# A hybrid decoder layer: four edits of the mixers' order, and the second norm's transposes of token tiles 1 and 3 at other places

## The chip, the cores and the metric

The kernel runs on one core of a Trainium2 chip. The metric is the device time of one execution in microseconds (us). The kernel before took 745.96 us, the median of three runs (744.57 to 748.39). Five engines work side by side: PE multiplies matrices into PSUM banks, DVE, ACT and POOL do element-wise work, and SP issues the transfers (DMA).

## The reference

One layer of a decoder trunk for 512 tokens of 1024 features, in float32.

```
x1  = x  + gate1 * out_proj(concat(FoX, RWKV7, MoBA))    # of in_proj(adaLN(RMSNorm(x)))
x2  = x1 + gate2 * down(silu(conv3(up_g)) * conv3(up_v)) # of adaLN(RMSNorm(x1))
out = RMSNorm(x2)

FoX  : softmax(q k / 8 + F_t - F_s), causal, 4 heads of 64
RWKV7: S_t = S_(t-1) diag(w_t) - (S_(t-1) kk_t)(kk_t a_t)^T + v_t k_t^T,  y_t = S_t r_t, 8 heads of 64
MoBA : causal attention in the own block of 256 keys and in the best past blocks, 4 heads of 64
```

The adaLN shifts, scales and gates are products of a conditioning vector with weights of their own. The hidden width of the gated MLP is 2816.

## The kernel before

**Products.** A float32 product is made of three matmuls: weights and data are each split into a high and a low part, and high by high, low by high and high by low are summed in PSUM. The input projection is cut into *units* of one contraction step each (three matmuls, L459 to L461, 128x128 weights against 512 tokens), the output projection likewise (L957 to L959). The class `Feed` hands them out: `feed.run(n)` issues the next n units, `feed.until(name)` issues units until the chunk of that name is done. It runs ahead with the weights of the chunks that follow: a transfer to `w_st`, a cast on ACT (`w_hi`, L229) and a subtraction on POOL or DVE (`w_lo`, L231). With each unit it also takes one step off `feed.side`, the list of small jobs beside: `mod2_steps` (32 steps, each a transfer of `w_m` and a DVE multiply, L434), then for each half `gate_steps` (eight steps, DVE L412 and L414), `gate_parts` (L420, L421), three empty steps and `gate_end` (two matmuls, L425).

**RWKV preparation.** For four pairs of heads j, `norm_cols(j)` spreads the norms over the partitions (one matmul, L529) and `k_prep(j)` builds the operands on DVE, ACT and POOL: `kk` (L632), `kt` (POOL, L635), `av` (L636), the first half of `KR` (L637), the two halves of `BK` (L639, L642), `rk` (L641) and the second half of `KR` (L643). `k_cols(j, q)` scales `BK` on POOL (`BKs`, L653) and turns it on PE (L658). `grams(j, par)` multiplies `BK` by `KR` into two banks, `at` and `ch` (L672), and DVE masks each of them into `AG` (L674). In the loop over j stand, in this order, `r_prep` (L665), `k_cols(j, 0)`, `grams(j, 0)`, one unit, `k_cols(j, 1)`, `grams(j, 1)` and two units.

**Recurrence.** It goes over eight chunks `cc` of 64 tokens. In each, PE multiplies `AG` by the state `vs` (L1092), starts the outputs (L1098), solves (L1108; ACT and DVE L1110 copy the result), and makes the next state (L1118), which DVE adds per parity (L1121) before L1092 of the next chunk can start. Between these stand attention steps (scores L1001 to L1005 into `at` banks, softmax on DVE and ACT, turning on PE L1019 into `mm` banks, copied as `ptr` L1021) and units, by the list `PAT`: an attention step and a unit, the same again, one unit, nothing. The first unit of a tile takes a new `mm` bank, of which there are two, shared with L1019. After chunk 4 the MoBA heads begin, and their scores need all their queries and keys: `feed.until` then issues what is missing, and DVE forms the last piece (`mk`, L735).

**Second norm.** `tail` adds the last contraction steps of the output projection for one token tile (three matmuls a step). `norm2_sum` adds to the residual and scales the rows; `norm2_cols(i)` turns token tile i on PE (L1226, two `mm` banks), shifts and scales it on ACT (L1234) and DVE (L1231), casts the high part on ACT (L1238) and subtracts the low part on POOL (L1239). The first up products (`up`) take token tiles 0 and 1 for four row blocks into two `ch` and two `at` banks, then tiles 2 and 3: 16 matmuls with the high part of the data (L1430, L1431) and 8 with the low part (L1433), each of 256 columns.

**What sets the order.** In the mixers PE runs in the order in which the program is written; the order on the other engines is made by a scheduler from the data and from priorities. From the second norm's first step to the first up products all engines run in the written order.

Of the kernel before, what the change touches and what calls it, by code (L numbers as in the profile page):

```python
# [14 lines left out]
OP = mybir.AluOpType  # L15
# [53 lines left out]
MP = ['', '2', '2']  # L69
PT = 3  # L70
GE = 3

SEVEN = (7, 9, 11, 13, 15)
NA = 16
# [66 lines left out]
def hybrid_trunk(ctx, tc, x, vecs, convs, mod_cols, mod_gates, in_first, in_cols, in_fox, in_moba, fox_f_bias, lora,  # L141
# [350 lines left out]
    with mix:  # L492
# [38 lines left out]
        with tc.tile_pool(name="prep", bufs=1) as pp:  # L531
# [98 lines left out]
            def k_prep(j):  # L630
                kk[j] = pp.tile([P, T], F32, name="kk", bufs=1)
                V.scalar_tensor_tensor(kk[j], kt[j], col("k_k", j), pnr[j], op0=OP.mult, op1=OP.mult)  # L632
                t1 = pp.tile([P, T], F32, name="t1", tag="sq", bufs=SQ)
                S.activation(t1, av[j], AF.Identity, scale=col("k_a", j), bias=omka[:, j:j + 1])
                G.tensor_tensor(kt[j], kt[j], t1, op=OP.mult)  # L635
                V.tensor_tensor(av[j], av[j], kk[j], op=OP.mult)  # L636
                V.tensor_tensor(KR[:, j, :, 0, :], c3(kk[j]), Pv[j][:, :, 0:64], op=OP.mult)  # L637
                BK[j] = pp.tile([P, 8, 3, 64], F32, name=f"BK{j}")
                V.tensor_tensor(BK[j][:, :, 0, :], c3(av[j]), c3(sv[j]), op=OP.mult)  # L639
                rk[j] = pp.tile([P, T], F32, name="sq", bufs=SQ)  # L640
                V.scalar_tensor_tensor(c3(rk[j]), KR[:, j, :, 1, :], col("r_k", j), c3(kt[j]), op0=OP.mult, op1=OP.mult)  # L641
                V.tensor_tensor(BK[j][:, :, 1, :], c3(kt[j]), c3(sv[j]), op=OP.mult)  # L642
                V.tensor_tensor(KR[:, j, :, 1, :], KR[:, j, :, 1, :], Pv[j][:, :, 1:65], op=OP.mult)  # L643
                S.copy(BK[j][H[1], :, 2, :], BK[j][H[1], :, 0, :])
# [22 lines left out]
            def grams(j, par):  # L667
                r = slice(64 * par, 64 * par + 64)
                for q in range(2):
                    pg = bank("ch" if q else "at", [P, 4, 2, 64])  # L670
                    for z in range(4):
                        mm(pg[:, z, :, :], BK[j][r, 4 * q + z, par:par + 2, :], KR[r, j, 4 * q + z, :, :],  # L672
                           start=True, stop=True)
                    V.tensor_tensor(AG[:, par, j, 4 * q:4 * q + 4, :].rearrange("p c (a t) -> p c a t", a=2), pg,  # L674
                                    mask[:, None, :, :].to_broadcast([P, 4, 2, 64]), op=OP.mult)

                for blk in range(2):
                    b = block(par, blk)
                    S.copy(AA[b, j], AG[b, par, j, :, 32 * blk:32 * blk + 32])


            norm_cols(0)
            k_prep(0)
            feed.until("r3")
            feed.run(LEAD[0])
            norm_cols(1)
# [3 lines left out]
            for j in range(4):  # L690
# [3 lines left out]
                k_cols(j, 0)  # L694
                for n, step in enumerate((lambda: grams(j, 0), lambda: feed.run(F1), lambda: k_cols(j, 1),
                                          lambda: grams(j, 1), lambda: feed.run(F2[j]), lambda: None)):
                    if n == KO and j < 2:
                        norm_cols(j + 2)
                        k_prep(j + 2)
                    step()  # L700
# [376 lines left out]


        v_tiles(0)
        feed.side += mod2_steps(w_m) + [mod2_end]  # L1080
        for half in range(2):
            feed.side += gate_steps(0, half, macc2, w_m) + [lambda half=half: gate_parts(0, half, m_part)]
            feed.side += [lambda: None] * GE + [lambda half=half: gate_end(0, half, bank("at"), g1b)]
# [1 line left out]
        for cc in range(NC_):  # L1085
# [42 lines left out]
            if cc > 5:  # L1128
                bonus(2 * cc - 12)
                bonus(2 * cc - 11)  # L1130
            fill(PAT[3])
        turn_bank[0] = "ch"
        gn_var(0)
        feed.run(G1)
# [130 lines left out]
    norm2_sum(1)  # L1265
    tail(2, 4, 5, 6, 7)
    norm2_cols(0)
    tail(3, 4, 5, 6)
    norm2_cols(1)
    tail(3, 7)  # L1270
    norm2_sum(2)
    norm2_sum(3)
    feed.run(UP2)
# [177 lines left out]
    for h in range(2):  # L1451
        for n, pu in enumerate(pfirst):
            feed.run(max(0, 6 + 2 * n - len(kept)))
            up(pu, kept[4 + 2 * n:6 + 2 * n], slice(256 * h, 256 * h + 256))
            if h == 0 and n < 2:
                norm2_cols(2 + n)
    us[0] = [conv(pu, NF * n) for n, pu in enumerate(pfirst[:2])]
    LATE.close()
    mixers.close()
# [118 lines left out]
```

## Time and profile before

| | |
|---|---|
| median of three runs | 745.96 us |
| the profiled execution | 745.82 us |
| its span, first to last instruction | 744.0 us |
| busy time of PE, DVE, ACT, POOL | 716.1, 484.3, 365.0, 311.6 us |
| mean granted clock of PE | 0.978 of full speed |

All durations below come from the one profiled execution, whose span lies 1.8 us below its time. A timeline row tells the start, the length and the instruction, and in square brackets how long the engine had been idle and who ended that. PE's matmuls overlap, so the distance from one start to the next tells more than a row's length. [...]

### The profile page before, as it was taken

To read this page: it belongs to the slowest core of one execution; us is meant where nothing else is said; L and a number is where in the kernel's file an instruction comes from. 1 tells how busy PE (TensorE), PEld (TensorE's weight loads), DVE (VectorE), ACT (ScalarE), POOL (GpSimd) and SP (SyncE) were. 2 spreads that over 40 slices of the span, in tenths; PEclk is the share of its full clock that TensorE was granted. 3 is DMA by queue.
4 is the path that set the end of the run, shared out by engine and by line. 5 is a ranking of instruction groups with operands and counts; after the bars stand their busy time and mean duration, and the time that the engine had idled before them with its cause. 6 is when DMAs were issued, how large, how long until landed. Compare 5 with 4: busy or idle time off the path is not lost.

```text
span 744.0 us, 11850 instructions
## 1 busy us (share of the span) xinstructions
PE 716.1 (96%) x4404; PEld 570.2 (77%) x4404; DVE 484.3 (65%) x833; ACT 365.0 (49%) x714; POOL 311.6 (42%) x264
## 2 busy tenths in 40 slices
PE   7999999999997999999999999999999999999996
PEld 5874767897665766677788888888888888888884
DVE  7957996876987567742639796788757683114104
ACT  8748655454432553645566545565563353223204
POOL 0023854664442312636576745454475432225210
PEclk9999989999977999999999999999999999999998
DMA  8941201237754141115234314323156633322203
GB/s 329 399 156 42 69 19 30 86 100 231 239 170 143 35 152 44 57 52 172 74 102 126 114 28 111 104 93 92 43 141 199 215 100 109 99 87 97 102 1 113
DMA packets 43021, 86.93 MB, mean 117 GB/s; under 512 B 5002, under 2 KB 5204, under 8 KB 42964
## 3 DMA queue, kind: packets, MB, share of 16 engines
q1 hardware_dynamic: 42963, 86.18, 36.0%
q8 instruction: 34, 0.56, 0.3%
q14 instruction: 24, 0.19, 0.1%
HBM read 84.05 MB, written 2.10 MB: 116 GB/s over the span
## 4 chain that ended last, share of the span: by engine, by line
PE 69%; DVE 15%; ACT 6%; issue 4%; POOL 3%; DMA 2%; SPq 0%; ACTq 0%; POOLq 0%; DVEq 0%
PE mm L459 3%; PE mm L460 3%; PE mm L461 2%; PE ch L378 2%; POOL w_lo L231 2%; PE ch L1188 2%; PE ch L1189 2%; PE ch L1187 2%; PE at L1315 2%; PE ch L1315 2%; PE at L1318 2%; PE at L1316 2%; DMA w_st<-in_w_up_dram 2%; PE ch L1318 2%; PE ch L1316 2%
## 5 line engine op out<-in xcount | busy, mean ns | idle before, releaser
L231 POOL TENSOR_TENSOR w_lo<-w_st,w_hi 128x512 fp32r<-128x512 f32 (+1 forms) x162 | 225.4, 1400 | 322.7 <-ACT w_hi L229 299.6
L229 ACT CAST w_hi<-w_st 128x512 fp32r<-128x512 f32 (+1 forms) x199 | 121.6, 618 | 157.1 <-PE at L1189 46.1
L231 DVE TENSOR_TENSOR w_lo<-w_st,w_hi 128x512 fp32r<-128x512 f32 x39 | 32.4, 832 | 72.8 <-ACT w_hi L229 72.7
L459 PE MATMUL mm<-h_hi,w_hi 128*128 128x512 f32 x104 | 49.4, 475 | 1.4 <-ACT ptr L1021 1.4
L460 PE MATMUL mm<-h_lo,w_hi 128*128 128x512 f32 x104 | 42.6, 410 | 0.0
L461 PE MATMUL mm<-h_hi,w_lo 128*128 128x512 f32 x104 | 42.6, 410 | 0.0
L1315 PE MATMUL ch<-h_hi,w_hi 128*128 128x512 f32 (+1 forms) x100 | 35.4, 363 | 0.7 <-ACT tm L1378 0.7
L1316 PE MATMUL ch<-h_hi,w_lo 128*128 128x512 f32 (+1 forms) x100 | 35.2, 361 | 0.0
L434 DVE SCALAR_TENSOR_TENSOR w_m<-w_m,cB 128x512 f32<-128x512 f32 x32 | 27.6, 886 | 9.3 <-DMA w_m<-in_mod_cols_dram 9.2
L1315 PE MATMUL at<-h_hi,w_hi 128*128 128x512 f32 (+1 forms) x88 | 32.4, 375 | 0.2 <-ACT tm L1378 0.2
L1316 PE MATMUL at<-h_hi,w_lo 128*128 128x512 f32 (+1 forms) x88 | 32.2, 372 | 0.0
L1008 DVE TENSOR_REDUCE mx<-at 128x1 f32<-128x128 f32 (+3 forms) x32 | 15.6, 488 | 18.9 <-PE at L1005 18.7
L1010 ACT ACTIVATE pr<-at,mx 128x128 f32<-128x128 f32 (+3 forms) x32 | 16.9, 527 | 21.8 <-DVE mx L1008 21.3
L459 PEld LDWEIGHTS mm<-h_hi,w_hi 128*128 128x128 f32 x104 | 20.6, 198 | 8.9 <-issue 3.1
L1444 ACT ACTIVATE tm<-tm 128x512 f32<-128x512 f32 x22 | 13.9, 632 | 27.5 <-DVE tm L1439 27.5
L1315 PE MATMUL mm<-h_hi,w_hi 128*128 128x512 f32 (+1 forms) x72 | 27.2, 382 | 0.0
L1316 PE MATMUL mm<-h_hi,w_lo 128*128 128x512 f32 (+1 forms) x72 | 27.1, 380 | 0.0
L461 PEld LDWEIGHTS mm<-h_hi,w_lo 128*128 128x128 f32 x104 | 20.6, 198 | 5.0
L1318 PE MATMUL ch<-h_lo,w_hi 128*128 128x512 f32 (+1 forms) x100 | 24.1, 363 | 0.0
L460 PEld LDWEIGHTS mm<-h_lo,w_hi 128*128 128x128 f32 x104 | 20.8, 200 | 2.4
L1445 DVE TENSOR_TENSOR tm<-tm 128x512 f32<-128x512 f32 x22 | 21.9, 993 | 1.0 <-ACT tm L1444 0.4
L1318 PE MATMUL at<-h_lo,w_hi 128*128 128x512 f32 (+1 forms) x88 | 22.2, 374 | 0.0
(667 smaller groups left out, 2049.3 us busy)
## 6 DMA issues: line engine op xcount, KB each, us to landing
w_st<-in_w_up_dram SPq DMA_DIRECT2D x88, 256.0 KB, 2.6
w_st<-in_w_down_dram SPq DMA_DIRECT2D x44, 256.0 KB, 2.6
wm<-in_mod_cols_dram SPq DMA_DIRECT2D x16, 512.0 KB, 10.3
w_m<-in_mod_cols_dram SPq DMA_DIRECT2D x32, 256.0 KB, 3.8
w_st<-in_in_cols_dram SPq DMA_DIRECT2D x30, 256.0 KB, 2.7
w_m<-in_mod_gates_dram SPq DMA_DIRECT2D x16, 256.0 KB, 2.9
w_st<-in_w_out_dram SPq DMA_DIRECT2D x16, 256.0 KB, 2.7
tm<-in_mod_gates_dram SPq DMA_DIRECT2D x16, 256.0 KB, 4.6
```

The source lines that it names most:

```text
L229: (V.tensor_copy if hv[0] else S.copy)(hi[:, :n], st[:, :n])
L231: e.tensor_tensor(lo[:, :n], st[:, :n], f32(hi[:, :n]), op=OP.subtract)
L434: V.scalar_tensor_tensor(wm, wm, 1.0, cB[:, cols], op0=OP.mult, op1=OP.mult, accum_out=acc2[:, z, k, half:half + 1])
L459: mm(out[0], hi[:, z, :], hT_hi[:, k, :], start=k == 0, stop=False)
L460: mm(out[0], hi[:, z, :], hT_lo[:, k, :], start=False, stop=False)
L461: mm(out[0], lo[:, z, :], hT_hi[:, k, :], start=False, stop=k == NK - 1)
L1008: V.reduce_max(mx[:, 0:1], s_ps[:, :n], axis=AX.X, negate=True)
L1010: S.activation(pr[:, :n], s_ps[:, :n], AF.Exp, bias=mx[:, 0:1], accum_out=mx[:, 1:2])
L1315: mm(o, hi[:, k, :], x[0][k], start=start and k == 0, stop=False, skip_group_check=not start)
L1316: mm(o, lo[:, k, :], x[0][k], start=False, stop=False, skip_group_check=not start)
L1318: mm(o, hi[:, k, :], x[1][k], start=False, stop=k == 3, skip_group_check=not start)
L1445: V.tensor_tensor(uv, ug, uv, op=OP.mult)
```

## The change

- `k_prep` is cut in two. `k_prep2` holds what came from L639 on (`BK`, `rk`, the second half of `KR`, the copy). In the loop over j, `k_prep2(j + 1)` is issued where `norm_cols(j + 2)` and `k_prep(j + 2)` stood (behind the first `grams`), and these two are issued behind the second `grams`.
- The masking of the grams is written with a priority raised by `AGP` = 60.
- `SD` = 12 empty steps stand ahead of `mod2_steps` in `feed.side`.
- At the end of chunks 0 to 3 of the recurrence one unit is issued.
- In the second norm, tile 1 is turned after the first of tile 3's four tail steps, not after the third; tile 3 is turned after the third up product, not after the second.

```diff
--- before.py
+++ after.py
@@ -69,6 +69,8 @@
 MP = ['', '2', '2']
 PT = 3
 GE = 3
+AGP = 60
+SD = 12
 
 SEVEN = (7, 9, 11, 13, 15)
 NA = 16
@@ -635,6 +637,8 @@
                 G.tensor_tensor(kt[j], kt[j], t1, op=OP.mult)
                 V.tensor_tensor(av[j], av[j], kk[j], op=OP.mult)
                 V.tensor_tensor(KR[:, j, :, 0, :], c3(kk[j]), Pv[j][:, :, 0:64], op=OP.mult)
+
+            def k_prep2(j):
                 BK[j] = pp.tile([P, 8, 3, 64], F32, name=f"BK{j}")
                 V.tensor_tensor(BK[j][:, :, 0, :], c3(av[j]), c3(sv[j]), op=OP.mult)
                 rk[j] = pp.tile([P, T], F32, name="sq", bufs=SQ)
@@ -671,8 +675,9 @@
                     for z in range(4):
                         mm(pg[:, z, :, :], BK[j][r, 4 * q + z, par:par + 2, :], KR[r, j, 4 * q + z, :, :],
                            start=True, stop=True)
-                    V.tensor_tensor(AG[:, par, j, 4 * q:4 * q + 4, :].rearrange("p c (a t) -> p c a t", a=2), pg,
-                                    mask[:, None, :, :].to_broadcast([P, 4, 2, 64]), op=OP.mult)
+                    with tc.high_priority(offset=AGP):
+                        V.tensor_tensor(AG[:, par, j, 4 * q:4 * q + 4, :].rearrange("p c (a t) -> p c a t", a=2), pg,
+                                        mask[:, None, :, :].to_broadcast([P, 4, 2, 64]), op=OP.mult)
 
                 for blk in range(2):
                     b = block(par, blk)
@@ -681,6 +686,7 @@
 
             norm_cols(0)
             k_prep(0)
+            k_prep2(0)
             feed.until("r3")
             feed.run(LEAD[0])
             norm_cols(1)
@@ -694,7 +700,10 @@
                 k_cols(j, 0)
                 for n, step in enumerate((lambda: grams(j, 0), lambda: feed.run(F1), lambda: k_cols(j, 1),
                                           lambda: grams(j, 1), lambda: feed.run(F2[j]), lambda: None)):
-                    if n == KO and j < 2:
+
+                    if n == KO and j < 3:
+                        k_prep2(j + 1)
+                    if n == 4 and j < 2:
                         norm_cols(j + 2)
                         k_prep(j + 2)
                     step()
@@ -1077,7 +1086,7 @@
 
 
         v_tiles(0)
-        feed.side += mod2_steps(w_m) + [mod2_end]
+        feed.side += [lambda: None] * SD + mod2_steps(w_m) + [mod2_end]
         for half in range(2):
             feed.side += gate_steps(0, half, macc2, w_m) + [lambda half=half: gate_parts(0, half, m_part)]
             feed.side += [lambda: None] * GE + [lambda half=half: gate_end(0, half, bank("at"), g1b)]
@@ -1128,7 +1137,8 @@
             if cc > 5:
                 bonus(2 * cc - 12)
                 bonus(2 * cc - 11)
-            fill(PAT[3])
+
+            fill("1" if cc < 4 else PAT[3])
         turn_bank[0] = "ch"
         gn_var(0)
         feed.run(G1)
@@ -1265,9 +1275,9 @@
     norm2_sum(1)
     tail(2, 4, 5, 6, 7)
     norm2_cols(0)
-    tail(3, 4, 5, 6)
+    tail(3, 4)
     norm2_cols(1)
-    tail(3, 7)
+    tail(3, 5, 6, 7)
     norm2_sum(2)
     norm2_sum(3)
     feed.run(UP2)
@@ -1452,8 +1462,8 @@
         for n, pu in enumerate(pfirst):
             feed.run(max(0, 6 + 2 * n - len(kept)))
             up(pu, kept[4 + 2 * n:6 + 2 * n], slice(256 * h, 256 * h + 256))
-            if h == 0 and n < 2:
-                norm2_cols(2 + n)
+            if h == 0 and n % 2 == 0:
+                norm2_cols(2 + n // 2)
     us[0] = [conv(pu, NF * n) for n, pu in enumerate(pfirst[:2])]
     LATE.close()
     mixers.close()
```

Three places show what becomes of the order on the engines. Line numbers are those of each kernel; after the change L674 reads L679, the lines L632 to L643 read L634 to L647, L459 to L461 read L461 to L463, L1092 and L1098 read L1101 and L1107, L1003 reads L1012, L1226 reads L1236, and L1430 to L1433 read L1440 to L1443.

DVE before, from the masking of the first grams of j = 0; P_772 and s_730 belong to j = 2, `kv` at L511 to the projection.

```order
L674 TENSOR_TENSOR AG<-at,mask 128x512
L674 TENSOR_TENSOR AG<-ch,mask 128x512
L632 SCALAR_TENSOR_TENSOR kk<-kv,vec_107,at 128x512
L636 TENSOR_TENSOR a_731<-a_731,kk 128x512
L637 TENSOR_TENSOR KR<-kk,P_772 128x8x64
L639 TENSOR_TENSOR BK_945<-a_731,s_730 128x8x64
L641 SCALAR_TENSOR_TENSOR sq<-KR,vec_107,kv 128x512
L642 TENSOR_TENSOR BK_945<-kv,s_730 128x8x64
L643 TENSOR_TENSOR KR<-KR,P_772 128x8x64
L511 SCALAR_TENSOR_TENSOR kv<-mm,vec_107,kv 128x511
L674 TENSOR_TENSOR AG<-at,mask 128x512
L674 TENSOR_TENSOR AG<-ch,mask 128x512
```

DVE after, from the same instruction.

```order
L679 TENSOR_TENSOR AG<-at,mask 128x512
L679 TENSOR_TENSOR AG<-ch,mask 128x512
L679 TENSOR_TENSOR AG<-at,mask 128x512
L513 SCALAR_TENSOR_TENSOR kv<-mm,vec_107,kv 128x511
L679 TENSOR_TENSOR AG<-ch,mask 128x512
L634 SCALAR_TENSOR_TENSOR kk<-kv,vec_107,at 128x512
L638 TENSOR_TENSOR a_731<-a_731,kk 128x512
L639 TENSOR_TENSOR KR<-kk,P_772 128x8x64
L679 TENSOR_TENSOR AG<-at,mask 128x512
L643 TENSOR_TENSOR BK_1013<-a_731,s_730 128x8x64
L679 TENSOR_TENSOR AG<-ch,mask 128x512
```

The second grams of j = 0 are masked three and five rows after the first, not ten; the operations for j = 2 now stand among the maskings of j = 1.

PE before, from the last unit of chunk 3 to the first MoBA scores (`mk`, `mq`).

```order
L459 MATMUL mm<-h_hi,w_hi 128x512
L460 MATMUL mm<-h_lo,w_hi 128x512
L461 MATMUL mm<-h_hi,w_lo 128x512
L1092 MATMUL ch<-vs,AG 64x64 x8
L1098 MATMUL ch<-KR,vs 64x64 x8
L459 MATMUL mm<-h_hi,w_hi 128x512
L460 MATMUL mm<-h_lo,w_hi 128x512
L461 MATMUL mm<-h_hi,w_lo 128x512
L459 MATMUL mm<-h_hi,w_hi 128x512
L460 MATMUL mm<-h_lo,w_hi 128x512
L461 MATMUL mm<-h_hi,w_lo 128x512
L1003 MATMUL at<-mk_2432,mq_2152 128x128
```

PE after, the same stretch.

```order
L461 MATMUL mm<-h_hi,w_hi 128x512
L462 MATMUL mm<-h_lo,w_hi 128x512
L463 MATMUL mm<-h_hi,w_lo 128x512
L461 MATMUL mm<-h_hi,w_hi 128x512
L462 MATMUL mm<-h_lo,w_hi 128x512
L463 MATMUL mm<-h_hi,w_lo 128x512
L1101 MATMUL ch<-vs,AG 64x64 x8
L1107 MATMUL ch<-KR,vs 64x64 x8
L1012 MATMUL at<-mk_2352,mq_2118 128x128
```

One unit more stands ahead of the chunk's first product (there is one at each of the four chunk ends), and the two units between L1098 and the MoBA scores are gone.

PE before, where token tile 3 is turned: the end of the second up product (`ch`) and the start of the third (`at`).

```order
L1430 MATMUL ch<-h_hi,w_hi 128x256
L1431 MATMUL ch<-h_hi,w_lo 128x256
L1433 MATMUL ch<-h_lo,w_hi 128x256 x8
L1226 MATMUL mm<-ident,tm 128x128 x8
L1430 MATMUL at<-h_hi,w_hi 128x256
L1431 MATMUL at<-h_hi,w_lo 128x256
```

PE after, where token tile 3 is turned: the end of the third up product and the start of the fourth.

```order
L1440 MATMUL at<-h_hi,w_hi 128x256
L1441 MATMUL at<-h_hi,w_lo 128x256
L1443 MATMUL at<-h_lo,w_hi 128x256 x8
L1236 MATMUL mm<-ident,tm 128x128 x8
L1440 MATMUL at<-h_hi,w_hi 128x256
L1441 MATMUL at<-h_hi,w_lo 128x256
```

The 24 matmuls of the third product now stand ahead of the turning. Tile 1's eight transposes move six matmuls forward in the same way.

## Rows read from the trace of the kernel before

**Rows 1.** The page's first part: busy time, share, instructions of each engine.

```profile
PE 716.1 (96%) x4404; PEld 570.2 (77%) x4404; DVE 484.3 (65%) x833; ACT 365.0 (49%) x714; POOL 311.6 (42%) x264
```

**Rows 2.** Windows: length, busy time of each engine, PEclk, DMA share, GB/s.

```profile
97.45:104.28 6.83, 6.83 (x20) 3.96 (x18) 6.73 (x9) 4.05 (x8) 2.73 (x2) 0.50 0.16 39
203.27:213.51 10.24, 9.48 (x68) 6.16 (x66) 7.59 (x20) 2.68 (x8) 3.72 (x4) 0.50 0.53 174
227.16:230.57 3.41, 3.41 (x22) 2.64 (x22) 3.15 (x5) 0.38 (x1) 1.48 (x2) 0.50 0.62 178
233.99:240.81 6.82, 6.38 (x40) 4.85 (x41) 4.28 (x10) 1.67 (x6) 0.00 (x0) 0.50 0.48 153
...
187.70:207.50 19.80, 17.95 (x223) 12.84 (x222) 18.92 (x50) 8.99 (x26) 10.14 (x10) 0.89 0.67 211
213.90:226.40 12.50, 10.59 (x122) 7.10 (x120) 12.33 (x25) 5.01 (x13) 7.07 (x9) 1.00 0.55 172
```

**Rows 3.** Waits of PE: line, released by, total us, times, longest.

```profile
PE mm L459 <- ACT ptr L1021: 1.4, 2, 0.8
```

**Rows 4.** Timeline of PE in the grams: start, length, instruction, idle before.

```profile
92.51 0.49 PE L529 MATMUL at<-nrm_p,indR 32*128 32x512 f32 x1
94.28 0.89 PE L658 MATMUL ch<-ident,BKs 64*128 64x64 f32 x8 [0.39 <-POOL BKs L653]
96.64 1.36 PE L672 MATMUL at<-KR,BK 64*128 64x128 f32 x8 [1.46 <-DVE AG L674]
...
115.17 1.16 PE L672 MATMUL ch<-KR,BK 64*128 64x128 f32 x8 [0.97 <-DVE AG L674]
...
122.26 1.11 PE L672 MATMUL at<-KR,BK 64*128 64x128 f32 x8
```

**Rows 5.** Timeline of DVE in the grams stage.

```profile
89.88 1.78 DVE L637 TENSOR_TENSOR KR<-kk,P 128x512 f32<-128x512 f32 x1
...
96.50 0.68 DVE L674 TENSOR_TENSOR AG<-ch,mask 128x512 f32<-128x512 f32 x1
...
113.24 0.68 DVE L643 TENSOR_TENSOR KR<-KR,P 128x512 f32<-128x512 f32 x1
```

**Rows 6.** Timeline of POOL in the grams stage.

```profile
88.09 3.01 POOL L231 TENSOR_TENSOR w_lo<-w_st,w_hi 128x512 fp32r<-128x512 f32 x2
```

**Rows 7.** Timeline of PE in the recurrence, chunks 3 and 4.

```profile
225.53 0.30 PE L1092 MATMUL ch<-vs,AG 128*64 128x64 f32 x2 [1.34 <-DVE vs L1121]
226.48 0.68 PE L1092 MATMUL ch<-vs,AG 128*64 128x64 f32 x14 [0.65 <-DVE vs L1121]
...
228.10 0.79 PE L459 MATMUL mm<-h_hi,w_hi 128*128 128x512 f32 x1
...
232.60 0.30 PE L1003 MATMUL at<-mk,mq 128*128 128x128 f32 x1 [1.72 <-DVE mk L735]
...
241.31 0.69 PE L1118 MATMUL ch<-vs,BKT 128*64 128x64 f32 x16
```

**Rows 8.** Timeline of DVE in the recurrence.

```profile
224.25 0.74 DVE L414 SCALAR_TENSOR_TENSOR macc<-w_m,cact,macc 128x512 f32<-128x512 f32 x1
...
231.77 0.69 DVE L735 TENSOR_TENSOR mk<-mm,mk 64x512 fp32r<-64x512 f32 x1 [1.31 <-ACT mk L734]
```

**Rows 9.** Timeline of PE where the output projection begins.

```profile
300.92 0.50 PE L959 MATMUL mm<-w_hi,h_lo 128*128 128x512 f32 x1 [0.20 <-POOL h_lo L937]
```

**Rows 10.** Timeline of PE in the second norm.

```profile
367.97 0.39 PE L1430 MATMUL ch<-h_hi,w_hi 128*128 128x256 f32 x1 [1.35 <-ACT h_hi L1238]
376.63 1.16 PE L1226 MATMUL mm<-ident,tm 128*128 128x128 f32 x8 [1.60 <-ACT tm L1234]
...
385.20 1.08 PE L1433 MATMUL ch<-h_lo,w_hi 128*128 128x256 f32 x8
```

**Rows 11.** Timeline of DVE in the second norm.

```profile
363.84 1.36 DVE L1231 TENSOR_SCALAR tm<-mm,mod 128x128 f32<-128x128 f32 x4
```

**Rows 12.** Timeline of POOL in the second norm.

```profile
381.90 2.52 POOL L1239 TENSOR_TENSOR h_lo<-tm,h_hi 128x512 fp32r<-128x512 f32 x2
```

## The prediction, made before the changed kernel was run

> **What bounds the kernel now.** I read the page's busy times first: PE works 716.1 of 744.0 us [rows 1], so waits of PE can give back 27.9 us at most, and over the whole program the edits add and remove no PE instruction. Next come the windows, searched for a granted clock below 1. [...] The third view is PE's list of waits with the timeline around each. Ahead of the stretch at 97.45 stand waits of 0.39 and 1.46 us [rows 4], ahead of the one at 227.16 waits of 1.34 and 0.65, ahead of the one at 233.99 a wait of 1.72 [rows 7]; the wait of 0.97 at 114.20 [rows 4] and the one of 1.60 in the second norm [rows 10] have no such stretch behind them. So a wait here may cost itself, or itself and a half-clock stretch. Last I looked at who is late. In the grams it is DVE (the masking), in the recurrence DVE too: it works 18.92 of 19.80 us and 12.33 of 12.50 us, and idles only in the half-clock stretch between, 10.24 - 7.59 = 2.65 us [rows 2]. There DVE, not PE, will be the bound as soon as PE gets faster.
>
> The sum is made against the profiled execution, 745.82 us, which lies 0.14 below the median.
>
> **Grams.** PE's waits are 0.39, 1.46 and 0.97 [rows 4]. The order of DVE is the same up to the first two maskings, so these end when they did, the second at 96.50 + 0.68 = 97.18 [rows 5]. L529 (0.49 [rows 4]) no longer stands ahead of the turning at 94.28, which waits for POOL either way: its wait grows to 0.88. The second grams' first bank is, by the pool's turns, then another one that is free early; the other (`ch`) still waits for 97.18. Before, it followed the first bank's matmuls of 96.64 (1.36 long, with the overlap about 1.15), at 97.8; so 0.6 are won, and 0.49 are paid back with L529 behind it. The 0.97 at 114.2 go, as eight DVE operations no longer stand between the two pairs of maskings. That is -1.1; I take -1.0. The idle time ahead of 97.45 is about as long as before (0.88 and the wait for 97.18), so I let the half-clock stretch stand. Ends: 0, and 2.82 + 6.83/2 = -6.2, with all waits and the stretch gone.
>
> **Recurrence.** Four units come earlier, and of them the two that stood between L1098 and the MoBA scores are gone from there. These took 228.10 to 232.60 - 1.72 = 230.88 [rows 7], 2.78 us at half clock, so 0.70 each at full clock. I follow DVE, since it is the bound. Its last state sum released L1092 at 226.48. Of its 2.65 us of idle time I take 2.0 as going (the hand-over from PE to the sums remains); against that, one L414 (0.74) and `mk` (0.69) [rows 8] now stand among the sums of chunk 3, by the order: +1.43. So L1092 starts at 226.48 - 2.0 + 1.43 = 225.9, and with L1092 (0.68 long, some 0.6 without the overlap) and L1098 of the same size the scores stand at 227.1, not 232.60: `mk` is long done, and the wait of 1.72 and the two units are gone. From the scores to L1118 of chunk 4 it was 241.31 - 232.60 = 8.71, of which some 0.7 was one of the two waits for `ptr` (1.4 together [rows 3]); the unit that took a new bank there no longer starts a tile. I leave the half-clock stretch of 6.82 in this place, since L1092 still waits for DVE just ahead of it (PE was free at 225.53 - 1.34 = 224.2 before, and comes no later now). L1118 then comes at 227.1 + 8.0 = 235.1: -6.2. Two units are done besides that before were still to do: -1.4. One tile now begins right behind a turning in chunk 6: +0.7, as the two of before. Together -6.9. Ends: with no idle time of DVE regained, 8.71 unchanged and a half-clock stretch as long as the longest one (10.24, 1.7 more), -1.9; with all 2.65, no extra DVE work ahead and no half-clock stretch (6.38/2 = 3.2 less), -12.8.
>
> **Empty steps.** 12 units pass before the first L434. By the order on DVE these stand where they stood between the state sums, but for one; the transfers of `w_m` are not the late ones. I count 0; if they collide with the gate steps, it is the +1.43 above.
>
> **Start of the output projection.** It now begins one attention step behind the last input unit, not two. Its third matmul waited 0.20 for POOL already [rows 9]. Ends 0 and +1.4 (all that the two earlier units had won is waited off again); I take +0.3, being nearer to the row.
>
> **Second norm, tile 1.** Its eight transposes stand 6 matmuls (1.4 us) earlier, but need the banks of tile 0, which DVE reads until 363.84 + 1.36 = 365.20 [rows 11]. PE waits there rather than 1.35 us before L1430 [rows 10]. ACT and DVE get tile 1 at almost the same time, so the wait moves and does not shrink: 0, between -1.35 and +0.5 (if ACT turns to tile 1 later than it did).
>
> **Second norm, tile 3.** PE waited 1.60 for a bank [rows 10]. With 24 matmuls of the third product ahead (eight of the kind take 1.08 [rows 10], so about 3 us) the bank is free: -1.60. What is late next is POOL: L1433 started at 385.20 [rows 10], would now start at 383.6, and its last four matmuls need the second of POOL's two subtractions, whose pair ends at 384.42 [rows 12]; POOL is as busy as before, so it is not earlier. The first four take 0.5, to 384.1: a wait of 0.3. Term -1.3, ends 0 and -1.6. No transfer of these products is queued behind the moved transposes.
>
> **Sum.** -1.0 - 6.9 + 0.3 + 0 - 1.3 = -8.9, so 745.82 - 8.9 = 736.9; with the 0.14 of the median 737.1, and I say 737.0.
>
> **Rivals.**
> *The half-clock stretches go too.* In the grams the early `at` bank and in chunk 4 the missing wait of 1.72 would leave PE without the idle time that preceded them. For it: 0.97 and 1.60 us alone had no half-clock stretch behind them. Against it: the idle time at 94 to 97 is as long as ever, and DVE's floor stands. DVE allows some 2.8 of the grams' 3.4; in the recurrence it is 3.2: 737.0 - 2.8 - 3.2 = 731.0, where 2.8 is what DVE's own work leaves (its busy 6.73 of the 6.83 us there [rows 2] shows how close it is).
>
> *DVE eats it.* None of DVE's idle time is regained, the first half-clock stretch stays, and the waits simply come at L1092: the scores come at 229.1, 3.5 earlier, less 1.7 for a longer half-clock stretch; with -1.4 and +0.7 this is -2.5, the grams give 0, tile 3 -1.3, the output projection +0.3: 745.82 - 3.5 = 742.3. For it: DVE is full in [rows 2]. Against it: its order in the chunks is nearly that of before, and the 2.65 us are idle time that PE alone made.
>
> *Slower: the last grams wait for their operands.* `KR` of j = 3 (L643) was done at 113.24 + 0.68 = 113.92 [rows 5], 8.3 us before the grams at 122.26 [rows 4]. Now its seven operations are strewn among the maskings, and the last stands behind the maskings of j = 2. POOL works at the same time, and there an operation of the kind took 1.78, not 0.68 [rows 5, 6]: 1.1 more for each, 7.7 for seven, and three of j = 2 behind the same maskings, 3.3: 11.0 more. The room is 8.3, less the 1.0 that PE is earlier and 2.7 for four maskings now ahead of it: 4.6. PE would wait 6.4 and fall into a half-clock stretch of 6.83, 3.4 more: +9.8, with the rest (-7.9) 747.7, slower than before. It decides as soon as `KR` of j = 3 comes later than about 121.3. Against it: POOL worked only 2.73 of the 6.83 us from 97.45 [rows 2], so it can't meet them all.
>
> [...]
>
> *The edits do nothing.* The scheduler puts the raised maskings where the data allow, which at the first grams is where they were; the units and the second norm are fixed by PE's order, so of this rival only the grams' -1.0 remains, inside the range.
>
> **How the numbers follow.** Forecast 0.48 (734 to 740); half-clock stretches gone 0.18; DVE eats it 0.24 (740 to 745); slower 0.08; the edits without effect 0.02. A measurement of this kernel can tell about 0.5% from no change, which is below 742.2 or above 749.7. Faster: 0.48 + 0.18 + a half of 0.24 = 0.78, less 0.02 for the forecast's own tail, so 0.76. Slower by over 0.5%: a half of the slower case and a mishap, 0.06. The rest, 0.18, is the same. The range leaves out a part of the gain below 731 and the slower case: 731 to 744.
>
> **What would show it.** Right: no wait at L672 near 114; two half-clock stretches or one in the recurrence, not three; L1003 straight behind L1098 with no wait for `mk`; waits for `vs` at L1092 of chunk 4 still above 1 us; L1226 of tile 3 without its 1.60, and a short wait for `h_lo` at L1433. Wrong: a wait of grams or turning for `KR` or `BKs` of j = 3; DVE with idle time in chunks 2 to 4; three half-clock stretches there; a wait of over 1 us where the output projection begins.

## The result and the profile after

The changed kernel takes 736.93 us (median of 4 runs, 734.96 to 738.00), the kernel before 745.27 beside it: a ratio of 0.9879, 95% interval 0.9843 to 0.9915. The profiled execution took 735.99 us, its span 734.2. The page's first part (columns as in [rows 1]):

```profile
PE 709.0 (97%) x4404; PEld 565.1 (77%) x4404; DVE 479.4 (65%) x833; ACT 365.0 (50%) x714; POOL 312.7 (43%) x264
```

PE is busy 7.1 us less, with the same 4404 matmuls. Its busy time at half clock fell from 26.1 us [rows 2] to the 9.62 shown below, which by itself would give 8.2 if the same work took half as long at full clock. That estimate is a little high: matmuls of 512 columns start 0.43 us apart in the changed kernel's half-clock stretch (102.00, 102.43, 102.86) and 0.23 behind it (108.29, 108.52). The other 2.7 of the span's 9.8 us are idle time of PE. The starts of the same instructions in the two timelines of PE tell where the difference arises:

| start of (name in the kernel before) | before | after | difference |
|---|---|---|---|
| first grams (L672, j = 0) | 90.58 | 91.17 | +0.59 |
| last grams (L672, j = 3) | 125.38 | 125.44 | +0.06 |
| MoBA scores (L1003) | 232.60 | 225.89 | -6.71 |
| L1118 of chunk 4 | 241.31 | 231.01 | -10.30 |
| L1108 of chunk 7 | 264.22 | 255.48 | -8.74 |
| tile 0 turned (L1226) | 361.62 | 352.55 | -9.07 |
| first up product (L1430) | 367.97 | 359.60 | -8.37 |
| first product behind the up products of the norm (L1315) | 394.60 | 385.19 | -9.41 |
| last PE instruction | 736.36 | 726.55 | -9.81 |

So 0.5 us came in the grams, 8.8 in the recurrence, 0.3 up to the second norm; 0.7 were lost ahead of the first up product, 1.0 won behind it and 0.4 up to the end. The 0.59 of the first row lies ahead of every edit. In the recurrence the gain was 10.4 up to L1118 of chunk 4, and 1.6 of it were lost again by the end of chunk 7. The windows of the half-clock stretch in the grams and of chunks 0 to 4, which answer to [rows 2]; the number behind the busy times is the clock that PE was granted, as a share of full speed:

```profile
96.07:106.31 10.24, 9.62 (x34) 5.97 (x34) 6.73 (x9) 3.66 (x8) 4.46 (x3) 0.50 0.09 26
185.58:231.01 45.43, 42.49 (x513) 31.00 (x513) 42.36 (x104) 20.18 (x55) 20.47 (x22) 1.00 0.68 212
```

Before the program's last few microseconds one half-clock stretch is left, in the grams, and it is longer (10.24 us for 6.83); the recurrence has none. Before, the same piece of program (from L1092 of chunk 0 to L1118 of chunk 4) read:

```profile
185.52:241.31 55.79, 49.49 (x506) 35.20 (x507) 47.09 (x112) 20.79 (x57) 20.63 (x22) 0.82 0.58 185
```

PE's idle time there went from 55.79 - 49.49 = 6.30 to 45.43 - 42.49 = 2.94, its busy time from 49.49 to 42.49, though two units more now lie in it. The waits of PE for DVE in the recurrence, answering to [rows 3], first the one for the state sums in the kernel before:

```profile
PE ch L1092 <- DVE vs L1121: 3.1, 4, 1.3
```

```profile
PE ch L1101 <- DVE vs L1130: 2.1, 4, 1.0
...
PE mm L1028 <- DVE mqb L741: 0.9, 1, 0.9
PE ch L1127 <- DVE vs L1119: 0.9, 1, 0.9
```

None for `ptr` and none for `mk`; the one for `mqb`, another evacuation of an `mm` bank, and the one for L1119 (the copy of chunk 1's solution) are new. The timelines of PE in the grams and in the recurrence, where [rows 4] and [rows 7] stood:

```profile
94.89 0.89 PE L662 MATMUL ch<-ident,BKs 64*128 64x64 f32 x8 [0.81 <-POOL BKs L657]
...
97.84 2.07 PE L676 MATMUL ch<-KR,BK 64*128 64x128 f32 x8 [0.61 <-DVE AG L679]
...
122.32 1.11 PE L676 MATMUL at<-KR,BK 64*128 64x128 f32 x8
```

```profile
212.67 0.33 PE L1101 MATMUL ch<-vs,AG 128*64 128x64 f32 x2 [0.20 <-DVE vs L1130]
...
224.67 0.68 PE L1101 MATMUL ch<-vs,AG 128*64 128x64 f32 x14 [0.43 <-DVE vs L1130]
...
225.89 0.33 PE L1012 MATMUL at<-mk,mq 128*128 128x128 f32 x1
...
231.01 0.69 PE L1127 MATMUL ch<-vs,BKT 128*64 128x64 f32 x16
...
234.09 1.14 PE L1101 MATMUL ch<-vs,AG 128*64 128x64 f32 x16 [1.03 <-DVE vs L1130]
```

In the grams 0.81 and 0.61 are left of 2.82, and nothing is waited for near 114. In chunk 4 the scores follow L1107 at once (225.89). The wait of 1.03 in chunk 5 is new; 1.55 of the 1.6 us lost behind chunk 4 are lost at that product. DVE in the grams [rows 5]:

```profile
96.51 0.68 DVE L679 TENSOR_TENSOR AG<-at,mask 128x512 f32<-128x512 f32 x1
97.11 0.68 DVE L679 TENSOR_TENSOR AG<-ch,mask 128x512 f32<-128x512 f32 x1
...
113.87 1.80 DVE L639 TENSOR_TENSOR KR<-kk,P 128x512 f32<-128x512 f32 x1
...
120.75 0.67 DVE L647 TENSOR_TENSOR KR<-KR,P 128x512 f32<-128x512 f32 x1
```

The two first maskings end at 97.79, as far behind the first grams as before (6.6 us). The second half of `KR` of j = 3 ends at 120.75 + 0.67 = 121.42, 0.9 ahead of the grams that need it, where it had 8.3 to spare. The start of the output projection [rows 9] and the second norm [rows 10]:

```profile
289.05 0.50 PE L966 MATMUL mm<-w_hi,h_hi 128*128 128x512 f32 x1 [0.38 <-ACT h_hi L945]
...
290.31 0.50 PE L968 MATMUL mm<-w_hi,h_lo 128*128 128x512 f32 x1 [0.54 <-POOL h_lo L946]
```

```profile
355.89 0.65 PE L1236 MATMUL mm<-ident,tm 128*128 128x128 f32 x4 [1.63 <-ACT tm L1244]
356.89 0.66 PE L1236 MATMUL mm<-ident,tm 128*128 128x128 f32 x4 [0.34 <-DVE tm L1241]
...
359.60 0.38 PE L1440 MATMUL ch<-h_hi,w_hi 128*128 128x256 f32 x1
...
369.34 0.93 PE L1236 MATMUL mm<-ident,tm 128*128 128x128 f32 x7
...
374.95 0.67 PE L1443 MATMUL ch<-h_lo,w_hi 128*128 128x256 f32 x4
376.11 0.74 PE L1443 MATMUL ch<-h_lo,w_hi 128*128 128x256 f32 x4 [0.49 <-POOL h_lo L1249]
```

The output projection waits 0.38 and 0.54 instead of 0.20. Tile 1 waits 1.63 and 0.34 for tile 0's banks, and the wait of 1.35 ahead of the first up product is gone. Tile 3 is turned without a wait (369.34), and L1443 waits 0.49 for POOL.

### The profile page after: what moved, and what is told of

It reads as the page before. It is cut to its first block, busy times and chain, and to the rows that moved or that the text cites. A ratio compares the mean times of both kernels' runs of the same rounds, so it can differ in the third digit from the quotient of the medians.

```text
span 734.2 us, 11846 instructions
## 1 busy us (share of the span) xinstructions
PE 709.0 (97%) x4404; PEld 565.1 (77%) x4404; DVE 479.4 (65%) x833; ACT 365.0 (50%) x714; POOL 312.7 (43%) x264
## 4 chain that ended last, share of the span: by engine, by line
PE 76%; DVE 10%; DMA 5%; issue 3%; ACT 3%; POOL 2%; SPq 0%; DVEq 0%; POOLq 0%; ACTq 0%
PE ch L1325 3%; PE ch L1328 3%; PE ch L1326 3%; DMA w_m<-in_mod_cols_dram 3%; PE at L1325 2%; PE at L1328 2%; PE at L1326 2%; PE mm L461 2%; PE ch L380 2%; PE mm L1328 2%; PE mm L1325 2%; PE mm L1326 2%; PE ch L1198 2%; PE ch L1199 2%; PE ch L1197 2%
## 5 line engine op out<-in xcount | busy, mean ns | idle before, releaser
L233 POOL TENSOR_TENSOR w_lo<-w_st,w_hi 128x512 fp32r<-128x512 f32 (+1 forms) x162 | 226.2, 1404 | 324.2 <-ACT w_hi L231 300.3
L233 DVE TENSOR_TENSOR w_lo<-w_st,w_hi 128x512 fp32r<-128x512 f32 x39 | 32.4, 832 | 72.9 <-ACT w_hi L231 72.7
L461 PE MATMUL mm<-h_hi,w_hi 128*128 128x512 f32 x104 | 47.4, 456 | 0.0
L463 PE MATMUL mm<-h_hi,w_lo 128*128 128x512 f32 x104 | 41.6, 400 | 0.0
L436 DVE SCALAR_TENSOR_TENSOR w_m<-w_m,cB 128x512 f32<-128x512 f32 x32 | 27.4, 878 | 10.2 <-DMA w_m<-in_mod_cols_dram 10.1
L461 PEld LDWEIGHTS mm<-h_hi,w_hi 128*128 128x128 f32 x104 | 19.8, 191 | 6.8 <-issue 3.1
L463 PEld LDWEIGHTS mm<-h_hi,w_lo 128*128 128x128 f32 x104 | 19.8, 190 | 4.7
L1325 PEld LDWEIGHTS ch<-h_hi,w_hi 128*128 128x128 f32 x100 | 18.8, 188 | 4.0 <-ACT tm L1388 0.8
## 6 DMA issues: line engine op xcount, KB each, us to landing
wm<-in_mod_cols_dram SPq DMA_DIRECT2D x16, 512.0 KB, 10.4
```

The source lines that it names most:

```text
L233: e.tensor_tensor(lo[:, :n], st[:, :n], f32(hi[:, :n]), op=OP.subtract)
L436: V.scalar_tensor_tensor(wm, wm, 1.0, cB[:, cols], op0=OP.mult, op1=OP.mult, accum_out=acc2[:, z, k, half:half + 1])
L461: mm(out[0], hi[:, z, :], hT_hi[:, k, :], start=k == 0, stop=False)
L463: mm(out[0], lo[:, z, :], hT_hi[:, k, :], start=False, stop=k == NK - 1)
L1325: mm(o, hi[:, k, :], x[0][k], start=start and k == 0, stop=False, skip_group_check=not start)
```

## The experiments

Ratios are against the kernel before, run beside each, with 95% intervals. Single runs of one kernel lie 2 to 12 us apart, so tenths of a microsecond are read from traces and the sum of a change from medians.

**The change without its four units.**

```diff
-            fill("1" if cc < 4 else PAT[3])
+            fill(PAT[3])
```

> The changed kernel without the four units at the ends of chunks 0 to 3; all the rest of the change stays. Theory A (the units carry the gain: they stand in front of PE's waits for the state sums, and spare it the two units and the wait ahead of the MoBA scores): the waits for vs, the 1.7 us for mk and the half-clock stretches of the recurrence come back, L1118 of chunk 4 at about 241 instead of 231.0, the time 744 to 745.5. Rival B (the empty steps and the moved DVE work carry it): 737 to 739, no half-clock stretch between 200 and 241.

740.83 us (737.80 to 743.35, 6 runs), ratio 0.9925 [0.9900, 0.9951]: between the two. Its waits of PE for others in the recurrence:

```profile
PE ch L1101 <- DVE vs L1130: 3.5, 5, 1.3
...
PE mm L461 <- ACT ptr L1030: 1.8, 2, 1.1
PE at L1012 <- DVE mk L744: 1.6, 1, 1.6
```

The waits came back as A says, but only two half-clock stretches of 3.41 us with them (from 223.87 and from 230.70), and not the one of 10.24 at 203; L1127 of chunk 4 stands at 235.70, not at 241. The units carry part, not all.

**The four units alone,** the same line in the kernel before.

> The kernel before with the four units at the ends of chunks 0 to 3, and nothing else of the change. Theory A: no half-clock stretch in the recurrence, L1118 of chunk 4 at about 231, 736 to 737.5. Rival B: 743 to 745.

740.77 us (736.86 to 744.37, 8 runs), ratio 0.9925 [0.9897, 0.9953]; the profiled execution took 737.79. Its recurrence is that of the changed kernel to 0.1 us (130.1 from the last grams to L1108 of chunk 7; 130.0 there, 138.8 before), without a half-clock stretch. So A holds for the recurrence of this execution, and the median lies 3 us above it: other executions go another way. Their mean granted clock goes along with their times: 0.986 to 0.988 in the three of 742.4 to 744.4 us, 0.992 to 0.994 in the other five (736.9 to 741.5). The profiles of all kernels agree on the recurrence. The four without the units (the kernel before, the one above and two below) have half-clock stretches of 6.8 to 20.5 us in it; of the ten with the units seven have none, and three have one of 3.41 us.

**The same kernel once more,** for a second profile.

> The kernel before with the four units alone, once more: a second profile of the same kernel, whose eight times went from 736.9 to 744.4. If half-clock stretches come in one execution and not in another, this profile has other stretches than the first (one, 98.4 to 105.3) and a time that differs by half their length; if the order alone decides them, it has the same one and the times differ for another reason.

738.41 us. One window of each, the grams' half-clock stretch in the first and in the second profile:

```profile
98.42:105.25 6.83, 6.83 (x23) 3.90 (x23) 6.72 (x9) 3.88 (x7) 2.72 (x2) 0.50 0.14 39
```

```profile
95.35:105.59 10.24, 8.89 (x32) 5.96 (x33) 10.11 (x14) 4.32 (x9) 4.46 (x3) 0.50 0.10 26
```

The same instructions in the same order got a stretch of 6.83 us in one execution and of 10.24 in the other, and no other one in either before the last 6 us. The length does change from execution to execution. From the first grams to the last it took 34.77 us with the shorter one and 35.61 with the longer, so the 3.41 us more cost 0.8. The two times differ by only 0.6 us, though, and an execution of 744 was not caught in a profile: where such a one loses its clock stays open. What sets the length of a stretch no run here shows.

**The change with the old preparation** (`k_prep` whole, no raised priority).

```diff
-AGP = 60
+AGP = 0
-            def k_prep2(j):
...
-                    if n == KO and j < 3:
-                        k_prep2(j + 1)
-                    if n == 4 and j < 2:
+                    if n == KO and j < 2:
                         norm_cols(j + 2)
```

> The changed kernel with the preparation and the masking of the grams as before (k_prep whole, no raised priority). The traces give the grams stage 0.5 us of the gain, since a longer half-clock stretch (10.24 for 6.83 us) took back most of 1.4 us of waits. By that: about 737.4, the last grams 0.5 us later, the half-clock stretch 6.83 again. Rival (the split also decides what comes later): the recurrence shows other waits, 739 or more.

738.18 us (737.89 to 742.88, 5 runs), ratio 0.9924 [0.9890, 0.9958]. In its trace the grams' stretch is 6.83 us again and the last grams come 0.5 us later behind the first, both as expected; the recurrence is 0.7 us longer than in the changed kernel. Two of the five runs are 4 us above the others, at a mean clock of 0.983 and 0.985 against 0.987 to 0.994. The median lies between the two expectations.

**The preparation alone,** in the kernel before.

```diff
+AGP = 60
...
+                    if n == KO and j < 3:
+                        k_prep2(j + 1)
-                    if n == KO and j < 2:
+                    if n == 4 and j < 2:
```

> The kernel before with the split preparation and the raised priority, and nothing else of the change. The change without its four units came out at 740.8, 5.5 below the kernel before, of which the second norm can have brought some 1. If the grams carry the rest, 741 to 742.5; if they carry what the trace shows of them (0.5 to 1.4), 744.5 to 746.

742.27 us (739.69 to 742.94, 10 runs), ratio 0.9952 [0.9927, 0.9977]: 3.6 us, more than its stage shows. The grams gained 0.4 us in its trace, the recurrence 3.5. The half-clock stretches:

```profile
95.90:106.14 10.24, 9.33 (x33) 5.68 (x32) 6.41 (x9) 3.67 (x8) 4.29 (x4) 0.50 0.11 26
225.60:229.02 3.42, 2.89 (x8) 1.78 (x6) 2.62 (x4) 0.92 (x2) 1.13 (x2) 0.50 0.73 196
232.43:235.84 3.41, 3.41 (x31) 2.35 (x29) 2.69 (x6) 0.70 (x3) 0.00 (x0) 0.50 0.70 207
```

The one at 203 [rows 2] is missing, though the waits around it are there as before (0.74 for `vs`, 1.08 for `ptr`). That need not come from the grams: the kernel with the empty steps alone (below), whose grams are the old ones, has none at that place of the program either. The later products of L1092 in chunk 4 start 39.1 us behind the first of chunk 0 in both, for 41.0 in the kernel before: as far as these profiles tell, the 10.24 us at half clock were worth 1.8 us there and not half their length; without them PE's waits on the way are 1.2 to 1.4 us longer. Over the executions the clock does bear the gain out: the mean granted clock was 0.984 to 0.989 in these ten (0.987 on average) and 0.974 to 0.991 in the 29 of the kernel before (0.983). How the preparation does that I could not settle.

**The empty steps alone,** and **the change without them.**

```diff
-        feed.side += mod2_steps(w_m) + [mod2_end]
+        feed.side += [lambda: None] * 12 + mod2_steps(w_m) + [mod2_end]
```

> The kernel before with the 12 empty steps, and nothing else of the change. If the empty steps carry the 3 to 4 us of the change without its units that the grams and the second norm don't explain, 742 to 743; if they do nothing, as the prediction had it, 745 to 747.

745.76 us (743.93 to 749.74, 10 runs), ratio 1.0009 [0.9986, 1.0032]. With `SD = 0` in the changed kernel:

> The changed kernel with SD = 0, no empty steps ahead of mod2_steps. The prediction gave them nothing: 736.9, the chunks 0 to 4 as in the changed kernel. Rival (they keep DVE's side work out of the first chunks, or bring it too near to the end of the side list): over 1 us either way.

737.40 us (735.66 to 738.39), ratio 0.9893 [0.9853, 0.9934], chunks 2 to 7 within 0.25 us of the changed kernel's. They are worth nothing that can be measured. The profiled execution of the first (749.74) has four half-clock stretches, with the waits of the kernel before and nearly its program:

```profile
96.50:103.32 6.82, 6.20 (x22) 5.30 (x22) 6.71 (x8) 3.87 (x8) 3.84 (x3) 0.50 0.15 39
116.97:127.22 10.25, 10.25 (x39) 6.57 (x40) 2.08 (x4) 5.01 (x12) 1.04 (x1) 0.50 0.05 20
229.62:233.03 3.41, 3.27 (x33) 2.84 (x34) 3.25 (x5) 0.39 (x1) 2.13 (x2) 0.50 0.47 148
236.44:246.68 10.24, 9.56 (x72) 6.99 (x73) 6.55 (x15) 1.87 (x6) 0.00 (x0) 0.50 0.36 104
```

30.7 us, among them one from 116.97, behind the wait of 1.0 for the masking that had none behind it in [rows 4].

**DVE's work in the recurrence made small.**

```diff
-            V.scalar_tensor_tensor(wm, wm, 1.0, cB[:, cols], op0=OP.mult, op1=OP.mult,
+            V.scalar_tensor_tensor(wm[:, 0:64], wm[:, 0:64], 1.0, cB[:, T * half:T * half + 64], op0=OP.mult, op1=OP.mult,
```

> The changed kernel with DVE's 32 multiplies of mod2_steps over 64 columns instead of 512 (the sums of the second modulation take only these), the transfers as they are. If DVE bounds the recurrence, as the prediction said, PE's waits for DVE there (2.1 for vs at L1101, 0.9 for vs at L1127, 0.9 for mqb) go for chunks 2 to 4: 2 to 3.5 us less, 733.5 to 735. Rival (PE's own order bounds it, DVE is merely busy): under 0.7 us, 736.2 to 737.

738.52 us (736.14 to 739.10), ratio 0.9893 [0.9866, 0.9920]: no gain. The same 464 matmuls, from L1101 of chunk 0 to the MoBA scores, changed kernel first, then this one (columns as in [rows 2]):

```profile
185.58:225.89 40.31, 37.37 (x464) 27.22 (x464) 37.43 (x94) 18.77 (x51) 19.55 (x21) 1.00 0.67 212
```

```profile
184.94:225.54 40.60, 37.69 (x464) 27.29 (x465) 32.05 (x99) 18.11 (x50) 17.03 (x22) 1.00 0.75 238
```

DVE works 5.4 us less, both run at full clock, and PE is idle for 2.9 us in both. So DVE's load does not bound this stretch of the recurrence. What the traces show at its waits is the next operation in DVE's queue. Ahead of the state sum of chunk 2, DVE in the changed kernel and here:

```profile
210.41 1.81 DVE L436 SCALAR_TENSOR_TENSOR w_m<-w_m,cB 128x512 f32<-128x512 f32 x1
...
212.15 0.15 DVE L1020 RECIPROCAL mx<-mx 128x1 f32<-128x1 f32 x1
212.22 0.39 DVE L1130 TENSOR_TENSOR vs<-ch,mp 64x256 f32<-64x256 f32 x1
```

```profile
209.99 1.82 DVE L416 SCALAR_TENSOR_TENSOR macc<-w_m,cact,macc 128x512 f32<-128x512 f32 x1
211.74 0.15 DVE L1020 RECIPROCAL mx<-mx 128x1 f32<-128x1 f32 x1
211.81 0.39 DVE L1130 TENSOR_TENSOR vs<-ch,mp 64x256 f32<-64x256 f32 x1
```

A piece of side work of 1.8 us stands almost directly ahead of the sum (L1130) in both: where the multiplies became short, a gate step took their place. In the changed kernel a POOL subtraction (L233, 1.31 from 210.36) and another POOL operation (L1136, 1.06 from 211.62) ran beside it; the next L436 (213.41), beside two operations of POOL on 64x256 (L1111, 2.15 together from 213.46), took 0.69. In chunk 4 of this run two gate steps stand ahead of `mk` likewise, PE waits for it, and a half-clock stretch of 3.41 us begins at 228.03:

```profile
227.70 0.84 PE L1028 MATMUL mm<-ident,pr 128*128 128x128 f32 x4 [1.45 <-DVE mk L744]
```

No run changed DVE's order alone, so that this order is the cause is read from the traces and not shown by an experiment.

**Tile 1 turned at its old place.**

```diff
-    tail(3, 4)
+    tail(3, 4, 5, 6)
     norm2_cols(1)
-    tail(3, 5, 6, 7)
+    tail(3, 7)
```

> The changed kernel with token tile 1 turned at its old place, after the third of tile 3's tail steps. The traces put the move at a loss of 0.7 us (1.63 and 0.34 of waits for banks for the 1.35 it spared). By that 736.2, with L1440 0.7 us earlier; by the prediction, which gave the move 0, 736.9.

736.48 us (735.41 to 739.23), ratio 0.9889 [0.9846, 0.9932]. From tile 0's turning to the first up product it takes 6.92 us, 7.05 in the changed kernel: 0.1 and not 0.7. The units alone, with tile 1 at its old place, took 6.88 and 7.02 in their two profiles; the four kernels without the units took 5.93 to 6.35, among them the change without units (6.11), where tile 1 is at its new place. The 0.7 us go with the units and not with the move; why PE and the norm's chain meet less well then was not tried. In three other profiles with the move (without the empty steps, with the old preparation, and with one unit moved, below) a half-clock stretch of 3.41 us follows tile 1's waits; up to the first product behind the up products they take only 0.1 to 0.3 us more than the changed kernel (32.7 to 32.9 us for 32.6).

**Tile 3 turned at its old place.**

```diff
-            if h == 0 and n % 2 == 0:
-                norm2_cols(2 + n // 2)
+            if h == 0 and n < 2:
+                norm2_cols(2 + n)
```

> The changed kernel with token tile 3 turned at its old place, after the second up product. The 1.60 us of waiting for a bank come back and the 0.49 for h_lo goes: 1.0 us more, 737.9. Rival (later work hides it): 736.9.

737.44 us (736.96 to 738.79), ratio 0.9899 [0.9860, 0.9938].

```profile
367.38 1.13 PE L1236 MATMUL mm<-ident,tm 128*128 128x128 f32 x8 [1.60 <-ACT tm L1244]
```

The wait of 1.60 is back. From the first up product to the first product behind them it takes 26.59 us, 25.59 in the changed kernel, 26.63 before. The move is worth 1.0 us, too little for the medians. In the recurrence this profile has the wait of chunk 5 that the changed kernel has (1.03 there), and 2.4 us later a half-clock stretch begins, which the changed kernel has not:

```profile
231.85 1.14 PE L1101 MATMUL ch<-vs,AG 128*64 128x64 f32 x16 [1.02 <-DVE vs L1130]
```

```profile
234.28:237.69 3.41, 3.41 (x25) 2.55 (x25) 2.59 (x7) 1.20 (x4) 0.00 (x0) 0.50 0.02 5
```

**One unit, then both units, into the gap of the grams.**

```diff
-lambda: feed.run(F1)
+lambda: feed.run(F1 + (j == 0))
-F2 = (2, 2, 2, 0)
+F2 = (1, 2, 2, 0)
```

> The changed kernel with one of the two units behind the second grams of j = 0 moved ahead of the second turning, where PE waits 0.81 for POOL and 0.61 for the masking. If the idle time ahead of it brings the half-clock stretch, as in all four stretches of the kernel before, the stretch of 10.24 us goes with it: 0.7 to 1.4 of waits and up to 5 of half clock, 731 to 735. Rival (the unit only changes places with the wait, and DVE's masking sets the pace): 736 to 737.5, and the half-clock stretch stays.

734.96 us (734.59 to 736.20), ratio 0.9861 [0.9816, 0.9907]. The wait for POOL is covered, the one for the masking grew:

```profile
97.36 1.56 PE L676 MATMUL ch<-KR,BK 64*128 64x128 f32 x8 [1.11 <-DVE AG L679]
```

The stretch behind it is 6.83 us for 10.24, and the grams end 1.1 us earlier. The median, the lowest of all, lies in the range of the first expectation, but the picture is the rival's: the wait moved and the stretch stayed. A stretch of 6.83 also came without the moved unit, in the profiles without the empty steps and with tile 3 at its old place, whose grams are those of the changed kernel. The profiled execution is the longest of the four (736.20) and has two more stretches of 3.41 us, behind the wait of chunk 5 and in the second norm. The ratio's interval takes in the changed kernel's 0.9879. With both units moved (`F1 + 2 * (j == 0)`, `F2 = (0, 2, 2, 0)`) and tile 1 at its old place:

> The changed kernel with both units behind the second grams of j = 0 moved ahead of the second turning, and token tile 1 turned at its old place. If PE's 0.81 and 0.61 of idle time in the grams are thereby covered, nothing idle stands ahead of 97 and the half-clock stretch of the grams goes: 1.4 + 3.4 to 5.1, and 0.7 from tile 1, 730 to 733. Rival (in the run with one unit moved, 1.1 of waiting and a stretch of 6.83 stayed; DVE's maskings come no earlier, so PE waits at another place): 734.3 to 736.

740.46 us (733.01 to 745.16, 12 runs), ratio 0.9918 [0.9886, 0.9950], which is that of the eleven runs up to 744.00: worse than with one, though the intervals overlap a little. PE in the grams of j = 0 and 2, POOL ahead of those of j = 2, and a window:

```profile
99.25 1.16 PE L676 MATMUL ch<-KR,BK 64*128 64x128 f32 x8 [0.99 <-DVE AG L679]
...
112.53 0.70 PE L662 MATMUL ch<-ident,BKs 64*128 64x64 f32 x5 [2.14 <-POOL BKs L657]
```

```profile
109.60 1.43 POOL L233 TENSOR_TENSOR w_lo<-w_st,w_hi 128x520 fp32r<-128x520 f32 x1 [4.05 <-ACT w_hi L231]
110.99 1.48 POOL L657 TENSOR_TENSOR BKs<-BK,PC 128x512 f32<-128x512 f32 x1
```

```profile
113.17:126.82 13.65, 13.65 (x55) 10.02 (x53) 5.22 (x8) 5.51 (x11) 4.20 (x4) 0.50 0.00 1
```

The half-clock stretch at 96 is gone, as hoped, and PE is far enough ahead to reach the turning of j = 2 before POOL, which has a weight subtraction in front of `BKs`: a wait of 2.14, and behind it the longest stretch of all, 13.65 us. Some 1.4 us of this profile's 742.24 come from another place: a stretch of 3.41 us at 10.76, ahead of every edit (the first grams start at 92.62, 91.17 in the changed kernel). The one execution with a mean clock of 0.999 took 733.01.

## Why the prediction was right, and where its steps were not

The time (737.0 forecast, 736.93 measured) and the direction were right; the terms were not all. That it fits to 0.1 us is luck: up to the end of chunk 7 the recurrence gained 8.8 us in the trace where its term had 5.5 (-6.2 and +0.7); the grams, the way from there to the second norm and the two turnings gave 2.3 less than their terms; and single executions went from 734.96 to 738.00.

- **Grams, -1.0.** The trace has -0.5. The waits went as worked out (2.82 to 1.42; the masking stayed as far behind the first grams, and the wait near 114 is gone), but "I let the half-clock stretch stand" does not hold for this execution: the stretch was 10.24 us for 6.83. It differs between executions: the four profiles without the units, without the empty steps, with tile 3 at its old place and with little DVE work have these grams with a stretch of 6.83 us. From the first grams to the last they take 33.4 to 33.5 us; the changed kernel takes 34.3, the kernel before 34.8. So the part gives 1.3 us in its stage with the old stretch and 0.5 with the longer one. Measured alone, it is worth 3.6 us of the median, by one trace most of it in the recurrence. That effect no step of mine had; its mechanism is open.
- **Recurrence, -6.9.** The step that failed is "I follow DVE, since it is the bound". L1092 of chunk 4 came at 224.67, not 225.9, with a wait of 0.43 and not over 1 us, and the run with little DVE work showed no gain. "I leave the half-clock stretch of 6.82 in this place" failed too: none came, which is 3.2 us by the estimate I gave for it. The wait in chunk 6 (+0.7) did not come. Against that, a wait of 1.03 in chunk 5, which I had not foreseen, cost 1.55. At the end of chunk 7 two units more were done, as forecast, but of the 1.4 us that this was to give back by the second norm only 0.3 came; 0.7 went into the waits where the output projection begins. The parts about `mk`, the two units and `ptr` were right. By the run alone, the units are worth 5.6 us of the median. The two ends of this term do not come out of the parts named for them: these give -2.5 and -12.2, not -1.9 and -12.8.
- **Empty steps, 0:** right, 1.0009 alone.
- **Output projection, +0.3:** 0.92 of waits for 0.20, which is +0.7, within its ends.
- **Tile 1, 0:** right, and my reading of the trace after (a loss of 0.7 by the move) was wrong.
- **Tile 3, -1.3:** measured -1.0, the wait for POOL being 0.49 and not 0.3.

The parts measured alone add up to about the whole: 3.6 for the preparation, 5.6 for the units, -0.7 for the empty steps, against 9.0 (0.0121 of 745.27) for all of them, each within 2 to 3 us either way; the second norm was not measured alone. Taken out of the whole change, the units and the preparation are worth 3.4 and 3.3 (0.9925 and 0.9924 for 0.9879).

Of the rivals, the half-clock stretches went in the recurrence, as one had it, and stayed in the grams; the 2.8 us that I left it there is no sum, since DVE's busy 6.73 of 6.83 us leave 0.1. The slower one came within 0.9 us: `KR` of j = 3 ended at 121.42. My limit for it, 121.3, had PE 1.0 us earlier than it came, so no wait followed. Of the seven operations that the rival put at 1.78 each, only the first half of `KR` (1.80 from 113.87, beside a POOL subtraction of 1.75 from 113.37) and the first half of `BK` (1.34 from 117.02, beside POOL's `kt`, 1.28 from 116.53) took longer than 0.75. What decides how long an operation of DVE takes beside one of POOL no run shows. The rival's picture, operands late and a half-clock stretch behind the wait, is what the one profile with both units moved shows, by way of POOL (a wait of 2.14, a stretch of 13.65).

## What to carry to other kernels

Independent matmuls are worth trying directly ahead of a product that waits for a short chain through other engines. Where an idle PE is followed by a stretch at half clock, they can save more than the wait: up to chunk 4 of this recurrence PE lost 3.4 us of idle time and 7.0 of busy time. A DVE that is busy 93% of the time need not be the bound: here it worked 37.43 of 40.31 us, and with 32.05 the same matmuls took 40.60. Ask what stands directly ahead of the late operation. Filling the gap of the grams with both units moved PE into the next late operand, with a wait of 2.14 for `BKs`: look at that margin before filling the second gap.

## What the hardware showed that I had not expected

Ahead of the program's last 7 us, half-clock stretches came in lengths of 3.41, 6.83 and 10.24 us (all three in the kernel before) and 13.65 (with both units moved), with different lengths at the same place in two executions of one kernel (6.83 and 10.24, the four units alone). The same waits had a stretch behind them in one profile and none in another: the 0.74 us ahead of 203 in the kernel before (10.24 us behind it) and with the preparation alone (none), the 1.0 us of chunk 5 with tile 3 at its old place (3.41 us behind it) and in the changed kernel (none). In these profiles the stretches are thus not a price of one wait, and a sum over them can only be given for many executions.
